# Fifteen and fourteen of 22 pairs by seven products, sums of activations made during `up`, and moves by GpSimd's queue

## The chip, the core and the metric

The kernel runs on one core of one Trainium2 chip. The metric is the device time of one execution in microseconds; what the host does to lay out arrays before the launch is not part of it. Five engines work beside one another, each on its own list of instructions in order: TensorE (PE; its weight loads are shown as PEld), VectorE (DVE), ScalarE (ACT), GpSimd (POOL) and SyncE (SP). DMA transfers are issued from the lists of SP, ACT or GpSimd and carried by 16 DMA engines that all of them share. TensorE writes to PSUM; the other operands lie in SBUF, 128 partitions wide.

## The reference

One encoder block on x of 256 tokens by 2048 features, in float32:

```python
hn = rmsnorm(h, mix_norm_pre)
z, xbc, dt_raw, u = split(hn @ w_in)                 # 2048 -> 1024, 1536, 32, 1024
mix = concat([ssd_mixer(z, xbc, dt_raw, ...), pool_mixer(u, ...)]) @ w_out
h = h + rmsnorm(mix, mix_norm_post)
gate, val = split(rmsnorm(h, ffn_norm_pre) @ w_up)   # 2048 -> 2 x 5632
ff = (gelu(dwconv(gate)) * val) @ w_down             # 5632 -> 2048
h = h + rmsnorm(ff, ffn_norm_post)
h = h + rmsnorm(sigmoid(rmsnorm(h, ple_norm_pre) @ w_ple_gate) * (p @ w_ple), ple_norm_post)
```

All six large weights together are 204 MB in float32, each read once or, in parts, twice.

## The kernel before

**Precision.** Every large product is made of three: an operand is split into a high part in the reduced float32 format that TensorE takes (`hi`, a cast on ScalarE, L152) and the rest (`lo`, a subtraction on VectorE, L153); the sum hi·hi + hi·lo + lo·hi is accumulated. `split` does this for 1024 columns of weights at a time, into a ring of five pairs of buffers. The raw weights come through a ring of three buffers of 1 MiB (`raw`). Larger tiles (128 x 2048, 1 MiB) come from one pool of 13 `page`s, half-size ones from three `mid`s.

**Stages.** In order: `dtu` (part of `w_in`), `xbc`, `z` with the two mixers between, `wo` (`w_out`), `up` (11 groups `s` of 512 gate and 512 value columns), `dn` (`w_down`, two halves of 1024 columns, 22 pairs of 128 rows each), `gt` (the gate, two halves, 8 pairs each), and the end. `up` computes features by tokens (`feature_pairs`: 64 matmuls per call, an l.h.s. of high weights with 512 columns of activations, high and low side by side, then low weights with 256). `dn` and `gt` compute tokens by features (`token_major`): a regular pair is 2 k-tiles x 2 token halves x 2 column halves x 3 products = 24 matmuls of 512 columns.

**Seven products.** For the pairs named in `fast`, `seven_products` (L239) does the 2 x 2 block product of a pair by seven block products instead of eight (Winograd's form): 21 matmuls. It needs sums of the activations' blocks, `s1` to `s4` (`pair_sums`, L774: four small VectorE operations, a cast, a subtraction), and sums of the weights' blocks (`add_blocks`, L232: three additions). After the last fast pair `combine` (L269) puts the seven accumulators together. In `dn` the fast pairs are 12 of 22 in each half; in the gate 2 of 8 in each.

**What is made ahead.** The block sums of the weights of all these 28 pairs are made during `up`, by `block_sums`: `fetch` loads the pair (1 MiB) into a page, `add` makes the sums two slots later, `store` writes them to device memory in the slot after. A slot is one half of a `feature_pairs` call; `work` is the list of jobs per slot, and `aside()` runs the next entry. Two of the 28 stay in SBUF. In `dn` a fast pair then loads the three raw blocks it still needs (0.75 MiB) and, unless held, its block sums (1 MiB, tile `dn..t`). The sums of activations are made in `dn` itself by `hid_sums`, just before they are used: at each fast pair of the first half, and again in the second but for four pairs (`dn_keep`), whose sums stay in two pages.

**Order and queues.** The instructions of each engine follow the program's text, shifted where a planner finds them ready earlier. All loads and stores are on SP's queue (`load`, L119), in program order, apart from the very first two (ACT's) and the low half of the gate's first block, which GpSimd's queue adds onto a negated copy (`first_gate`, L943). `at` tells before which pair of the second half of `dn` the residual `h` is loaded back (`back`, 13) and that block is prepared (`first_gate`, 16). In `up` GpSimd multiplies the convolved gate by the token factors `rfb` (L885), 11 times.

Of the kernel before, what the change touches and what calls it, by code (L numbers as in the profile page):

```python
# [51 lines left out]
def build(nc, a, out):  # L52
    x = a["x"][0]
    w_in, w_out, w_up = a["w_in"][0], a["w_out"][0], a["w_ffn_up"][0]
    w_down, w_gate, w_ple = a["w_ffn_down"][0], a["w_ple_gate"][0], a["w_ple"][0]
    out = out[0]

    with tile.TileContext(nc) as tc, \
# [37 lines left out]
        c_dt = DSSD + 1536  # L96
        r0 = wp.tile([P, 2048], F32, tag="raw", bufs=3, name="dtur0")
        for n in range(2):
            first = ins(nc.scalar.dma_start(r0[:, n * 352:(n + 1) * 352],
                                            w_in[:P, c_dt + n * 352:c_dt + (n + 1) * 352]))  # L100
# [55 lines left out]
        def raw(name, src, a_, b_):  # L156
            r = wp.tile([P, 2048], F32, tag="raw", bufs=3, name=name)
            if src is None:
                return r
            last["dma"] = load(r[:, :a_ * b_].rearrange("p (a b) -> p a b", a=a_), src, True)  # L160
            return r
# [46 lines left out]
        def block_sums(name, w, c0, k, held):  # L208
# [30 lines left out]
        def seven_products(name, stage, w, k0, c0, a_, acc, alt, start, stop):  # L239
# [3 lines left out]
            if (stage, c0, k0) in sums_:  # L243
                r = raw(f"{name}r", None, 0, 0)
                last["dma"] = load(r[:, 512:1536], w[(k0 + 1) * P:(k0 + 2) * P, c0:c0 + 1024], True)
                last["dma"] = load(r[:, :512], w[k0 * P:(k0 + 1) * P, c0:c0 + 512], True)
# [6 lines left out]
            else:  # L253
                r = t = raw(f"{name}r", w[k0 * P:(k0 + 2) * P, c0:c0 + 1024]
                            .rearrange("(k p) c -> p k c", p=P), 2, 1024)
# [35 lines left out]
        def token_major(name, w, c0, ks, get, acc, tail=1, fast=(), alt=None, sums=None, at=()):  # L291
# [3 lines left out]
            for u in range(nu):  # L295
# [3 lines left out]
                if u in fast:  # L299
                    if u == fast[0]:  # L300
# [3 lines left out]
                r = None if f"{name}{k0}_0" in ready else raw(f"{name}r{k0}", w[k0 * P:(k0 + 2) * P, c0:c0 + 1024]  # L304
                                                               .rearrange("(k p) c -> p k c", p=P), 2, 1024)
# [17 lines left out]
        def feature_major(name, w, c0, get, acc):  # L323

            for u in range(4):
                r = raw(f"{name}r{u}", w[u * 512:(u + 1) * 512, c0:c0 + 512]
                        .rearrange("(k p) c -> p k c", p=P), 4, 512)
# [12 lines left out]
        def feature_pairs(name, w, c0, get, acc):  # L340
# [102 lines left out]
        for u in range(0, NK, 2):  # L443
            r = [wp.tile([P, 2048], F32, tag="raw", bufs=3, name=f"dtur{u}") if u else r0, page(f"dtur{u + 1}")]
            for j in range(2):
                k = u + j
                if k == 0:
                    last["dma"] = load(r[0][:, 704:1056], w_in[:P, c_dt + 704:c_dt + 1056])
# [3 lines left out]
                for c0, c1 in ((0, 704), (704, 1056)) if k == 1 else ((0, 1056),):  # L452
                    last["dma"] = load(r[j][:, c0:c1], w_in[k * P:(k + 1) * P, c_dt + c0:c_dt + c1])
# [59 lines left out]
        load(pmat.rearrange("p (g s t) -> p g s t", g=4, s=2),  # L513
# [565 lines left out]
```

## Time and profile before

| what | value |
|---|---|
| median of 3 runs | 1123.38 us (1123.28 to 1124.6) |
| profiled execution, its time | 1123.11 us |
| profiled execution, its span (first to last instruction) | 1121.3 us |
| granted TensorE clock, mean | 0.997 |
| DMA | 300.87 MB, 268 GB/s over the span |

A row of a group reads: line of the kernel, engine, operation, output<-inputs by tile name, shapes, count | busy us, mean ns of one | idle time of the engine just before, and what ended it. A row by stretches reads: stretch in us, its length, busy time and number of instructions for PE, PEld, DVE, ACT and POOL, then granted clock, mean busy share of the 16 DMA engines, and GB/s. In the chain of work, a piece is start, length, engine, tile and line. A row of a DMA issue has its size and the time from issue to landing. Matmuls are pipelined: one of 512 columns is shown as about 393 ns long, but starts 231 ns after the one before it.

### The profile page before, as it was taken

The page shows a single profiled execution, that of the slowest core. Times are in us where ns is not written, and L with a number is a line of the kernel's source. Part 1 is how long each engine was busy: PE and PEld are TensorE (multiplying, and loading weights), DVE is VectorE, ACT ScalarE, POOL GpSimd, SP SyncE. Part 2 cuts the span into 40 slices and gives each one's busy share as a digit, 9 for nine tenths or more (in the row PEclk, how much of TensorE's full clock was granted, in tenths as well). Part 3 has the DMA queues.
Part 4 walks back from the last instruction along what each step waited for, and adds up shares of the span by engine and source line. Part 5 has one row for each costly group of instructions (what it writes and reads, how often), then busy time and mean ns, then how long its engine had stood idle before and what let it go on. Part 6 is the DMA issues. An engine that isn't in the chain of part 4 may idle for free.

```text
span 1121.3 us, 15775 instructions
## 1 busy us (share of the span) xinstructions
PE 1109.1 (99%) x5971; PEld 956.4 (85%) x5971; DVE 925.2 (83%) x1275; ACT 663.9 (59%) x927; POOL 76.2 (7%) x86
## 2 busy tenths in 40 slices
PE   9999999999999999999999999999999999999996
PEld 9999987888888888888888888888888888888875
DVE  6569895799898877877877768888899999889795
ACT  6847663555764554554545445445677777786672
POOL 0200004200110100000000000000000000001001
PEclk9999999999999999999999999999999999999998
DMA  9862447456789989989999898996969688995663
GB/s 363 310 207 96 170 161 269 151 188 190 252 308 347 328 300 336 314 289 309 333 330 314 276 330 289 325 304 224 339 185 334 221 286 301 383 318 177 230 235 109
DMA packets 145996, 300.87 MB, mean 268 GB/s; under 512 B 5504, under 2 KB 98560, under 8 KB 137856
## 3 DMA queue, kind: packets, MB, share of 16 engines
q1 hardware_dynamic: 145360, 298.45, 78.6%
q0 software_dynamic: 272, 1.05, 0.5%
q8 instruction: 47, 0.77, 0.3%
q10 hardware_dynamic: 288, 0.36, 0.1%
q14 instruction: 29, 0.24, 0.1%
HBM read 268.38 MB, written 31.46 MB: 267 GB/s over the span
## 4 chain that ended last, share of the span: by engine, by line
PE 96%; ACT 1%; DVE 1%; issue 1%; POOL 1%; POOLq 0%; DVEq 0%; ACTq 0%
PE va L87 22%; PE ga L87 21%; PE dna L87 14%; PE woa L87 7%; PE xbc L87 6%; PE gt L87 5%; PE dtu L87 4%; PE z L87 4%; PE dns L87 3%; PE dn0s L87 1%; PE dn1s L87 1%; PE ple L87 1%; PE pw L87 1%; PE yd L87 0%; PE gts L87 0%
## 5 line engine op out<-in xcount | busy, mean ns | idle before, releaser
L87 PE MATMUL ga<-wox,ug_0h 128*128 128x512 f32 x352 | 125.5, 395 | 0.0
L87 PE MATMUL ga<-wox,ug_1h 128*128 128x512 f32 x352 | 125.1, 394 | 0.0
L87 PE MATMUL va<-wox,uv_1h 128*128 128x512 f32 x352 | 124.8, 393 | 0.0
L87 PE MATMUL va<-wox,uv_0h 128*128 128x512 f32 x352 | 124.8, 393 | 0.0
L87 PE MATMUL ga<-wox,ug_1l 128*128 128x256 f32 x352 | 99.1, 282 | 0.0
L87 PE MATMUL ga<-wox,ug_0l 128*128 128x256 f32 x352 | 99.1, 282 | 0.0
L87 PE MATMUL va<-wox,uv_1l 128*128 128x256 f32 x352 | 99.1, 281 | 0.0
L87 PE MATMUL va<-wox,uv_0l 128*128 128x256 f32 x352 | 99.1, 281 | 0.0
L87 PEld LDWEIGHTS va<-wox,uv_1h 128*128 128x128 f32 x352 | 66.1, 188 | 15.0
L87 PEld LDWEIGHTS va<-wox,uv_0h 128*128 128x128 f32 x352 | 66.1, 188 | 15.0
L87 PEld LDWEIGHTS ga<-wox,ug_0h 128*128 128x128 f32 x352 | 66.1, 188 | 14.9
L87 PEld LDWEIGHTS ga<-wox,ug_1h 128*128 128x128 f32 x352 | 66.1, 188 | 14.9
L87 PEld LDWEIGHTS ga<-wox,ug_0l 128*128 128x128 f32 x352 | 66.2, 188 | 0.1
L87 PEld LDWEIGHTS ga<-wox,ug_1l 128*128 128x128 f32 x352 | 66.2, 188 | 0.0
L87 PEld LDWEIGHTS va<-wox,uv_0l 128*128 128x128 f32 x352 | 66.2, 188 | 0.0
L87 PEld LDWEIGHTS va<-wox,uv_1l 128*128 128x128 f32 x352 | 66.2, 188 | 0.0
L885 POOL TENSOR_TENSOR fc<-fc,rfb 128x1024 f32<-128x1024 f32 x11 | 28.0, 2547 | 438.6 <-ACT fc L884 438.6
L87 PE MATMUL dna<-dn_0h,hs 128*128 128x512 f32 x160 | 50.1, 393 | 0.0
L87 PE MATMUL dna<-dn_1h,hs 128*128 128x512 f32 x160 | 49.9, 393 | 0.0
L235 DVE TENSOR_TENSOR dnb<-dnb 128x1024 f32<-128x1024 f32 x24 | 30.8, 1283 | 17.8 <-DMA dnb<-w_ffn_down 17.6
L903 ACT CAST hs<-hid 128x512 fp32r<-128x512 f32 x44 | 27.2, 617 | 23.2 <-PE dna L87 14.8
L904 DVE TENSOR_TENSOR hs<-hid,hs 128x512 fp32r<-128x512 f32 x44 | 30.2, 686 | 9.8 <-ACT hs L903 9.7
(1903 smaller groups left out, 3105.3 us busy)
## 6 DMA issues: line engine op xcount, KB each, us to landing
dnb<-w_ffn_down SPq DMA_DIRECT2D x24, 1024.0 KB, 10.4
dns<-dnb SPq DMA_DIRECT2D x22, 1024.0 KB, 7.4
dn0r<-w_ffn_down SPq DMA_DIRECT2D x10, 1024.0 KB, 6.0
dn1r<-w_ffn_down SPq DMA_DIRECT2D x10, 1024.0 KB, 7.1
zr<-w_in SPq DMA_DIRECT2D x8, 1024.0 KB, 5.1
dtur<-w_in SPq DMA_DIRECT2D x14, 528.0 KB, 8.7
wo0r<-w_out SPq DMA_DIRECT2D x7, 1024.0 KB, 5.6
wo1r<-w_out SPq DMA_DIRECT2D x6, 1024.0 KB, 5.5
```

The source lines that it names most:

```text
L87: last["pe"] = ins(nc.tensor.matmul(o, lhsT, rhs, start=start, stop=stop, skip_group_check=True))
L235: nc.vector.tensor_add(v[:, 0:2], v[:, 0:2], v[:, 1::2])
L885: nc.gpsimd.tensor_tensor(cv.rearrange("p (f t) -> p f t", f=4), cv.rearrange("p (f t) -> p f t", f=4), rfb.unsqueeze(1).to_broadcast([P, ...
L903: nc.scalar.copy(t[:, :512], src)
L904: nc.vector.tensor_sub(t[:, 512:], src, t[:, :512].bitcast(F32))
```

## The change

1. **More fast pairs.** `dn`: 15 pairs in the first half and 14 in the second by seven products; the gate: three in the first half and two in the second, five in all. In the gate's second half the order of the pairs is changed, so that its two fast pairs are two whose activation sums were made in the first half. There are now 34 pairs whose block sums are made in `up`; the spacing of these jobs goes from 3 slots to 2.4.
2. **Sums of activations made during `up`.** For ten pairs (`dn_stored`) `hid_sums_jobs` makes the sums as soon as the activations are there, in a job of `work`, and stores them to device memory (0.5 MiB each). In both halves of `dn` they are loaded into a `mid`. The other pairs' sums are made in `dn`, in both halves; no pages hold sums any more.
3. **GpSimd's queue.** `load_aside` issues from GpSimd's queue: fetches and stores of block sums, stores and loads of the sums of activations.
4. **Host tiles.** All large weights, `pool_w` and the pool matrix are laid out on the host as the tiles that are loaded: 128 rows of 8 KB each, one after another (`up` loaded rows of 1 KB, `xbc` 2 KB, the others 4 KB). The three raw blocks of a fast pair are parts of such a tile, rows of 4 and 2 KB.
5. **Order inside a fast pair.** The block sums' second half (`t42`) is split before the first (`t13`), and the products are in the order a11, a12, a22, s4, s2, s1, s3 (before: a11, a12, s4, s1, s3, a22, s2).
6. **Moved steps.** The multiplication by `rfb` in `up` goes from GpSimd to VectorE. In `dn`, `back` goes to pair 18, the first gate block is loaded at 19 (a step of its own, `first_load`) and prepared at 21. The pages of `vg` are taken when first written.

```diff
+        def load_aside(dst, src, ahead=True):
+            with tc.issue_after(last["dma"]) if not ahead else nullcontext():
+                return ins(nc.gpsimd.dma_start(dst, src))
...
 def block_sums(name, w, c0, k, held):
             def fetch():
                 r = page(f"{name}b{c0}_{k}")
                 pg.append(r)
-                load(r.rearrange("p (k c) -> p k c", k=2),
-                     w[k * P:(k + 2) * P, c0:c0 + 1024].rearrange("(k p) c -> p k c", p=P))
+                load_aside(r, w[c0 // 1024, k // 2], False)
...
-                    load(t, pg[0])
+                    load_aside(t, pg[0])
...
 def seven_products(name, stage, w, k0, c0, a_, acc, alt, start, stop):
-                last["dma"] = load(r[:, 512:1536], w[(k0 + 1) * P:(k0 + 2) * P, c0:c0 + 1024], True)
-                last["dma"] = load(r[:, :512], w[k0 * P:(k0 + 1) * P, c0:c0 + 512], True)
+                last["dma"] = load(r[:, 512:1536], w[c0 // 1024, k0 // 2][:, 1024:], True)
+                last["dma"] = load(r[:, :512], w[c0 // 1024, k0 // 2][:, :512], True)
...
+            t42 = split(f"{name}d", t[:, 1024:], 1024)
             t13 = split(f"{name}c", t[:, :1024], 1024)
-            t42 = split(f"{name}d", t[:, 1024:], 1024)
             for x, (wh, wl), c, o, own in (
-                    ("a11", b11, 0, alt[0], True), ("a12", b2, 0, acc[0][0], False), ("s4", b2, 512, acc[0][1], False),
-                    ("s1", t13, 0, alt[1], True), ("s3", t13, 512, alt[2], True), ("a22", t42, 0, acc[1][0], False),
-                    ("s2", t42, 512, alt[3], True)):
+                    ("a11", b11, 0, alt[0], True), ("a12", b2, 0, acc[0][0], False), ("a22", t42, 0, acc[1][0], False),
+                    ("s4", b2, 512, acc[0][1], False), ("s2", t42, 512, alt[3], True), ("s1", t13, 0, alt[1], True),
+                    ("s3", t13, 512, alt[2], True)):
...
 def feature_pairs(name, w, get, acc):
-                r = raw(f"{name}r{u}", w[u * 1024:(u + 1) * 1024, c0:c0 + 256]
-                        .rearrange("(k p) c -> p k c", p=P), 8, 256)
+                r = raw(f"{name}r{u}", w[u])
...
-        dn_fast, gt_fast, dn_keep = ((2, 3, 5, 7, 8, 10, 12, 13, 15, 16, 18, 19), (2, 3, 5, 7, 8, 10, 12, 13, 15, 16, 18, 19)), ((4, 6), (1, 2)), (3, 8, 13, 18)
-        gt_ks = list(range(NK)), [0, 1, 12, 13, 8, 9, 2, 3, 4, 5, 6, 7, 10, 11, 14, 15]
+        dn_fast, gt_fast = ((2, 3, 4, 5, 6, 8, 9, 10, 11, 13, 14, 15, 16, 18, 19), (2, 3, 4, 5, 6, 8, 9, 10, 13, 14, 15, 16, 18, 19)), ((4, 5, 6), (1, 2))
+        dn_stored = (2, 3, 4, 6, 9, 10, 13, 15, 16, 19)
+        gt_ks = list(range(NK)), [0, 1, 8, 9, 10, 11, 2, 3, 4, 5, 6, 7, 12, 13, 14, 15]
...
-                work[3 * i + 2 + j].extend(jobs)
+                work[12 * i // 5 + 3 + j].extend(jobs)
...
+        def hid_sums_jobs(k):
+            o = []
+            def make():
+                o.append(lp.tile([P, 1024], F32R, tag="hs", bufs=2, name=f"he{k}"))
+                hid_sums_of(k, o[0][:, 512:].bitcast(F32), o[0])
+            def store():
+                kept[k] = dp.tile([P, 1024], F32, tag=f"hsum{k}", bufs=1, name=f"hsum{k}")
+                load_aside(kept[k], o[0].bitcast(F32))
+            return [make], [store]
+        for u in dn_stored:
+            for j, jobs in enumerate(hid_sums_jobs(2 * u)):
+                work[u // 2 * 8 + u % 2 * 2 + 6 + j].extend(jobs)
...
-            nc.gpsimd.tensor_tensor(cv.rearrange("p (f t) -> p f t", f=4), cv.rearrange("p (f t) -> p f t", f=4),
+            nc.vector.tensor_tensor(cv.rearrange("p (f t) -> p f t", f=4), cv.rearrange("p (f t) -> p f t", f=4),
                                     rfb.unsqueeze(1).to_broadcast([P, 4, L]), op=ALU.mult)
...
 def hid_sums(k):
             (h1, l1), (h2, l2) = get_hid(k), get_hid(k + 1)
-            if k not in kept:
...
+            o = mid(f"hd{k}", F32R)
+            if k in kept:
+                load_aside(o.bitcast(F32), kept[k])
+                d = sums_in(o)
             else:
-                d = kept[k]
+                d = hid_sums_of(k, mid(f"hs{k}"), o)
...
+        def first_load():
+            first["r"] = page("gtf")
+            last["dma"] = load(first["r"], w_gate[0, 0])
...
-                      fast=dn_fast, sums=hid_sums, at={13: back, 16: first_gate})
+                      fast=dn_fast, sums=hid_sums, at={18: back, 19: first_load, 21: first_gate})
```

More of the change, by code (lines that the diff above doesn't have):

```diff
@@ L154, in split, with raw @@
             return hi, lo
-        def raw(name, src, a_, b_):
+        def raw(name, src=None):
             r = wp.tile([P, 2048], F32, tag="raw", bufs=3, name=name)
-            if src is None:
-                return r
-            last["dma"] = load(r[:, :a_ * b_].rearrange("p (a b) -> p a b", a=a_), src, True)
+            if src is not None:
+                last["dma"] = load(r, src, True)
             return r
@@ L871, in build, with hid_part, hid_sums_of @@
             for j, jobs in enumerate(block_sums(*w_, i >= len(which) - 2)):
-                work[3 * i + 2 + j].extend(jobs)
-        hid = []
+                work[12 * i // 5 + 3 + j].extend(jobs)
+        hid, kept = [], {}
+        def hid_part(k):
+            return hid[k // 8][:, (k % 8) * L:(k % 8 + 2) * L]
+        def hid_sums_of(k, s, o):
+            return pair_sums(f"he{k}", s, o, *(hid_part(k)[:, i * P:(i + 1) * P] for i in range(4)))
+        def hid_sums_jobs(k):
[10 more added lines that the diff above has]
+                work[u // 2 * 8 + u % 2 * 2 + 6 + j].extend(jobs)
         for s in range(DFF // 512):
@@ L941, in back @@
                 last["dma"] = load(h[t], h_kept[t])
+        first = {}
+        def first_load():
+            first["r"] = page("gtf")
+            last["dma"] = load(first["r"], w_gate[0, 0])
         def first_gate():
-            r, hi, lo = page("gtf"), page("gtfh", F32R), page("gtfl", F32R)
-            src = w_gate[:2 * P, :1024].rearrange("(k p) c -> p k c", p=P)
-            last["dma"] = load(r.rearrange("p (k c) -> p k c", k=2), src)
+            r, hi, lo = first["r"], page("gtfh", F32R), page("gtfl", F32R)
             nc.scalar.activation(lo, r, AF.Copy, scale=-1.0)
-            nc.gpsimd.dma_start(lo.rearrange("p (k c) -> p k c", k=2), src, accum_op=ALU.add)
+            nc.gpsimd.dma_start(lo, w_gate[0, 0], accum_op=ALU.add)
             nc.scalar.copy(hi, r)
@@ L963, in build @@
         gple = gload("gple", a["ple_norm_post"][0])
-        vg = [page(f"vg{t}") for t in range(2)]
+        vg = []
         sq = [[], []]
@@ L1023, in build @@
                         nc.scalar.activation(so, sv, AF.Square, accum_out=q)
+                    if half == n == 0:
+                        vg.append(page(f"vg{t}"))
                     nc.vector.tensor_mul(vg[t][:, c], v, gple[:, c])
```

77 lines of the change are left out of this document (38 added, 39 removed).

## The prediction

> **What bounds the kernel now.** I read the page first: the share of each engine and the chain of work that ended last.
>
> ```profile
> span 1121.3 us, 15775 instructions
> PE 1109.1 (99%) x5971; PEld 956.4 (85%) x5971; DVE 925.2 (83%) x1275; ACT 663.9 (59%) x927; POOL 76.2 (7%) x86
> DMA packets 145996, 300.87 MB, mean 268 GB/s; under 512 B 5504, under 2 KB 98560, under 8 KB 137856
> ...
> PE 96%; ACT 1%; DVE 1%; issue 1%; POOL 1%; POOLq 0%; DVEq 0%; ACTq 0%
> ```
>
> TensorE carries 96% of the chain, so a microsecond is gained by fewer matmuls, and lost by any new wait in front of one. The busy share of PE alone would not prove that it streams, so the second view is the chain in order of time (start, length, what):
>
> ```profile
> 319.91 22.33 PE va L87 x128
> ...
> 809.75 5.55 PE dna L87 x24
> ...
> 891.49 22.16 PE dna L87 x96
> ```
>
> A regular pair of `down` is 24 matmuls of 512 columns in 5.55 us; 96 take 22.16 us. One costs 0.231 us. The third view is the table by stretches: `up`, the two column halves of `down`, then two stretches of 20 us with high DMA traffic (columns: length, then busy time of PE, PEld, DVE, ACT, POOL, granted clock, DMA share, GB/s).
>
> ```profile
> 319.91:788.96 469.05, 469.05 (x2689) 411.74 (x2689) 378.05 (x479) 235.24 (x312) 28.01 (x11) 1.00 0.93 307
> 788.96:902.50 113.54, 113.54 (x493) 92.27 (x493) 105.23 (x146) 81.69 (x108) 0.00 (x0) 1.00 0.77 261
> 902.50:1016.74 114.24, 114.19 (x495) 92.40 (x494) 104.81 (x143) 84.60 (x109) 3.82 (x8) 1.00 0.91 323
> 960.00:980.00 20.00, 20.00 (x88) 16.26 (x87) 18.60 (x27) 14.84 (x18) 0.00 (x0) 1.00 0.97 372
> 20.00:40.00 20.00, 20.00 (x126) 20.00 (x125) 14.35 (x19) 15.56 (x21) 4.88 (x3) 1.00 1.01 398
> ```
>
> Each half of `down` has 12 fast pairs (21 matmuls) and 10 regular ones: 492 matmuls, 492 x 0.231 = 113.7 us, and the halves last 113.5 and 114.2 us. `Down` has no room between matmuls. But VectorE is busy 105 of 114 us beside it, and in the second half the DMA engines 91%: the cover over the cheaper matmuls is thin there, and this is where the change adds work.
>
> **The change, part by part.**
>
> *Fewer matmuls.* Fast pairs go from 12 and 12 to 15 and 14 in `down`, and from 4 to 5 in the gate: 6 more, each saving 3 matmuls: 18 x 0.231 = 4.16 us, all on the chain. Half 0 of `down` becomes 15 x 21 + 7 x 24 = 483 matmuls, 111.7 us; half 1 14 x 21 + 8 x 24 = 486, 112.4 us. The order of the seven products adds no matmul: 0.
>
> *VectorE in down.* Rows of VectorE in `down`, and some in order of time (start, length):
>
> ```profile
> L904 DVE TENSOR_TENSOR hs<-hid,hs 128x512 fp32r<-128x512 f32 x41 | 28.1, 686 | 9.1 <-ACT hs L903 9.0
> L153 DVE TENSOR_TENSOR dn_0l<-dn1r,dn_0h 128x1024 fp32r<-128x1024 f32 x10 | 12.2, 1219 | 2.2 <-ACT dn_0h L152 2.2
> L782 DVE TENSOR_TENSOR he<-hd,he 128x512 fp32r<-128x512 f32 x15 | 10.2, 683 | 0.7 <-ACT he L781 0.7
> ```
>
> ```profile
> 809.85 1.22 DVE L153 TENSOR_TENSOR dn010bl<-dn010r,dn010bh 128x1024 fp32r<-128x1024 f32 x1
> 810.99 0.68 DVE L904 TENSOR_TENSOR hs<-hid,hs 128x512 fp32r<-128x512 f32 x1
> 811.59 1.22 DVE L153 TENSOR_TENSOR dn010cl<-dn010t,dn010ch 128x1024 fp32r<-128x1024 f32 x1
> 812.72 0.28 DVE L777 TENSOR_TENSOR hd<-hid 128x128 f32<-128x128 f32 x1
> 812.93 0.28 DVE L778 TENSOR_TENSOR hd<-hid 128x128 f32<-128x128 f32 x1
> ```
>
> Instructions overlap at their ends: from start to start 1024 columns take 1.14 us, 512 take 0.60, 128 take 0.21 (0.31 behind a result just made). A regular pair costs 2 x 1.14 + 0.60 = 2.88 us of VectorE; a fast pair whose sums are at hand 0.60 + 3 x 1.14 + 0.60 = 4.62, under its 21 x 0.231 = 4.85 us of PE; one whose sums are made there about 1.5 more (four small ones and one of 512), 6.15, which is over. So "made" pairs live on the slack of others. Before: half 0 12 x 6.15 + 10 x 2.88 = 102.6 us, half 1 (four sums kept) 96.5. After, with ten pairs' sums loaded: 10 x 4.62 + 5 x 6.15 + 7 x 2.88 = 97.1 and 10 x 4.62 + 4 x 6.15 + 8 x 2.88 = 93.8. VectorE gets lighter by 5.5 and 2.7 us while PE loses 2.1 and 1.4: the cover holds, 0. ScalarE follows it at 82 to 85 of 114 us busy.
>
> *What up takes on.* Ten `pair_sums` at 1.5 us; block sums of 34 instead of 28 pairs; eleven multiplications by `rfb`, moved from GpSimd.
>
> ```profile
> L885 POOL TENSOR_TENSOR fc<-fc,rfb 128x1024 f32<-128x1024 f32 x11 | 28.0, 2547 | 438.6 <-ACT fc L884 438.6
> L235 DVE TENSOR_TENSOR dnb<-dnb 128x1024 f32<-128x1024 f32 x24 | 30.8, 1283 | 17.8 <-DMA dnb<-w_ffn_down 17.6
> ...
> dnb<-w_ffn_down SPq DMA_DIRECT2D x24, 1024.0 KB, 10.4
> dns<-dnb SPq DMA_DIRECT2D x22, 1024.0 KB, 7.4
> ```
>
> VectorE: 10 x 1.5 + 6 x (1.14 + 2 x 0.60) + 11 x 1.14 = 15 + 14 + 12.5 = 41.5 us, on 378 busy of 469: 420, 89%. PE covers it: 0, if the multiplication, which now waits for the Gelu in VectorE's own queue, finds splits ahead of it (between 0 and, at one of its 1.14 us for each of 11 groups, 12.5; I take 0, as the five buffers of split weights hold 5 x 16 matmuls, 14 us by the `va` row of 128 in 22.33). VectorE waited 17.6 us for fetched blocks in all and PE for none of it.
>
> *Queues.* 34 fetches, 32 stores, ten stores and twenty loads of sums pass SP's queue for GpSimd's, 96 issues. In `up` GpSimd then runs nothing else; SP's loads of weights no longer stand behind a fetch that waits for a page. Of GpSimd's queue there is one DMA in the trace, the low half of the gate's first block:
>
> ```profile
> gtfl<-w_ple_gate POOLq DMA_DIRECT2D x1, 1024.0 KB, 14.4
> ...
> gtf<-w_ple_gate SPq DMA_DIRECT2D x1, 1024.0 KB, 13.0
> ...
> dn126r<-w_ffn_down SPq DMA_DIRECT2D x1, 512.0 KB, 11.7
> ```
>
> 14.4 us there against 13.0 for its high half on SP in the same busy stretch. The same 1024 KB take SP 7.4 to 10.4 us in the rows above, so the queue costs between 0 and 7 us of landing time each; I take 1.4, the pair nearest to each other. In `up` a block is fetched two slots, 11 us, before its sum, and the wait that replaces it is VectorE's, covered as above. In `down` a load of sums must find a free buffer of three, two pairs (9.7 us) ahead: covered at 7 to 10 us, not at 14.
>
> *Host tiles.* `up` moves 307 GB/s at a share of 0.93, which is 330 at full share, most of it in rows of 1 KB (98560 packets are under 2 KB). The change adds 12 block moves of 1 MiB and ten of half: 17.8 MB, 38 GB/s, 345 in all: more than 330. Were the rows to stay, `up` would be bound by DMA. They become 8 KB; the stretch from 20 to 40 us, with rows of 4224 B, has 394 at full share. 345 fits: 0. The start (352 columns at a time, as before) is taken as unchanged: between -1 and +1 us, 0.
>
> *DMA in down.* A regular pair loads 1 MiB, a fast one 1.75 (0.75 if its block sum is held), loaded sums 0.5. Check on before: half 1 is 10 + 12 x 1.75 + 2 (`h` back) + 2 (gate) + 1 (`ple`) = 36 MiB, 37.7 MB, in 114.2 us: 330 GB/s, and the row has 323. After: half 0 7 + 13 x 1.75 + 2 x 0.75 + 5 = 36.25 MiB, 340 GB/s. Half 1: 8 + 24.5 + 5 + 2 + 2 + 1 = 42.5 MiB, 44.6 MB, in 112.4 us: 396 GB/s. The highest rows are 372 and 398; half 1 as it stands has 323 / 0.91 = 355 at full share. So the sum is close: at 398 it costs 0, at 372 (119.9 us) 7.5, at 355 13.2. I take 0.3, because not all is due inside the half. Three raw buffers mean that pairs 2 to 4 are loaded when pair 2 starts; from there 33.75 MiB, 35.4 MB, are left for 101 us: 350 GB/s, and 364 if all must land 4 us before use. That lies under 372, and more of it moves in 8 KB rows than before.
>
> *The later gate block.* `h` comes back at pair 18 instead of 13, the first gate block is fetched at 19 and split at 21 (both were 16).
>
> ```profile
> 978.41 1.91 ACT L948 ACTIVATE gtfl<-gtf 128x2048 fp32r<-128x2048 f32 x1
> 980.63 1.43 POOL L949 DMA_DIRECT2D gtfl<-w_ple_gate  x1 [203.62 <-ACT gtfl L948]
> 1005.26 0.39 PE L87 MATMUL dna<-dn_0h,hs 128*128 128x512 f32 x1
> 1022.92 0.63 PE L87 MATMUL gt<-gtfh,dnxh 128*128 128x512 f32 x2
> ```
>
> Now: pair 20 starts at 1005.3 and the gate at 1022.9. After, 3.5 us earlier (five of the six pairs): 1001.8, 1019.4. ScalarE ran this copy some 6 us ahead of pair 16; ahead of pair 21 (1007.3) that is about 1001, GpSimd issues at 1003, and with 14.4 us it lands at 1017.5, 2 us before use, where it had 28. Two copies of 1.9 us now stand on ScalarE in front of pair 21's splits. Between 0 and 5 us (a landing of 20); I take 0.1.
>
> *Gate 5.* One more fast pair makes three in a row (4, 5, 6) in the gate's first half: VectorE does four splits for two and makes one more pair's sums, 4.0 + 2.1 - 2.3 = plus 3.9 us, against PE minus 0.7, once. Around these pairs the table by stretches has
>
> ```profile
> 1034.00:1064.00 30.00, 30.00 (x132) 24.41 (x131) 22.62 (x32) 20.88 (x27) 1.85 (x6) 1.00 0.70 233
> ```
>
> 7.4 us of VectorE free: between 0 and, with no gap at the right place, 3.9 - 0.7 = 3.2; I take 0.1.
>
> *Sum.* -4.16 + 0.3 + 0.1 + 0.1 = -3.7. Span 1121.3 - 3.7 = 1117.6; the profiled run took 1123.11 us: 1119.4; the median of the three runs, 1123.38, is 0.27 above it: 1119.7.
>
> **The rivals.**
>
> *Down's second half is bound by DMA (slower).* For it: 396 GB/s asked on average, pairs 13 to 16 fast in a row with `h` and the gate block right behind, and landing times that already reach 11.7 us for half a MiB. Against: the stock of three raw buffers, PE without a gap at 372. At 372 for the whole half it is +7.5: 1127; it turns the sign under 44.6 / (112.4 + 4.2) = 383 GB/s if nothing is loaded ahead. The Trainium skill ("SBUF — State Buffer", "Summary: rules for kernel authors") says to reckon with about 358 GB/s for transfers from HBM. By that rule half 1 would take 124.6 us, +12.2, an estimate from that page. This case's trace does not hold to it: 372 and 398 stand above. Chance 0.17.
>
> *GpSimd's queue is late.* Loads of sums that take 14.4 us where 9.7 are given cost up to 4.7 each; the ones that stand third in a row of fast pairs, about six, cost up to 28. For it: one row of 14.4; against: that one reads and adds, at twice the size. With 1.5 each: 1128.7. The Trainium skill, in the same section of "SBUF — State Buffer", says that descriptor making for this queue is starved while VectorE is in one of its fast modes; the single row here, an issue of 1.43 us, shows no such delay. Chance 0.07.
>
> *The gate starts late.* The low half lands at 20 us: +3: 1122.7, no change that can be measured. Chance 0.12.
>
> **How the numbers follow.** My forecast, the stages keep their cover: 0.64, its own range 1117.7 to 1121.1. A measurement of this kernel tells 0.2% (2.2 us) from no change. Faster: 0.64 plus a small part of the late gate, 0.66; same: the rest of it, 0.10; slower: DMA and the queue, 0.24. The range of 8 in 10 starts at 1117.6 (start gains, no waits) and reaches to the DMA case at 1127.
>
> **What would show it.** Right: no gap between matmuls in `down`, halves of 111.7 and 112.4 us, `up` at a lower DMA share than 0.93 with more GB/s, VectorE there near 89%. Wrong: ScalarE waiting for `dn..t` or `dn..r` in half 1 with a DMA share over 1 (DMA); matmuls or `hd` behind a GpSimd DMA (queue); the first `gtfl` matmul alone in a gap at the gate (late block); a stretch of `up` longer than its 469 us, that VectorE or DMA has no cover there.

## The result and the profile after

The changed kernel takes 1142.29 us (1141.3 to 1143.9), the kernel before beside it on the same chip 1123.33: ratio 1.017, 95% interval 1.0158 to 1.0183. The profiled execution took 1142.01 us, span 1140.2, 18.9 more than before. The forecast was 3.7 less. The page of the changed kernel (engines, DMA, shares of the chain):

```profile
span 1140.2 us, 15963 instructions
...
PE 1112.3 (98%) x5953; PEld 955.1 (84%) x5953; DVE 939.8 (82%) x1317; ACT 671.4 (59%) x939; POOL 100.0 (9%) x171
DMA packets 57389, 333.90 MB, mean 293 GB/s; under 512 B 6368, under 2 KB 7264, under 8 KB 23520
...
PE 69%; DMA 13%; DVE 9%; issue 4%; ACT 3%; POOL 1%; DVEq 0%; POOLq 0%; ACTq 0%
```

TensorE had 96% of the chain and has 69%: transfers and VectorE now decide for stretches. The table by stretches (`up`, then about the two halves of `down`; columns as in the prediction):

```profile
319.75:801.00 481.25, 473.88 (x2691) 414.38 (x2690) 394.05 (x547) 235.10 (x321) 40.64 (x76) 0.99 0.89 342
801.00:914.00 113.00, 112.38 (x488) 91.13 (x488) 102.90 (x132) 86.17 (x110) 5.91 (x11) 1.00 0.88 322
914.00:1034.00 120.00, 114.47 (x485) 89.80 (x484) 102.25 (x125) 86.16 (x106) 6.77 (x13) 1.00 0.94 352
```

From the first matmul of one stage to the first of the next, the span splits as follows (us):

| stretch | before | forecast | after |
|---|---|---|---|
| `up` (first `va` to first `dn`) | 469.0 | 469.0 | 481.2 |
| `down`, `ple` and panel (to the first `gt`) | 234.1 | 231.1 | 239.3 |
| gate and end | 98.4 | 97.8 | 100.0 |

`Up` lost 12.1 us; `down` should have lost 3.5 us of matmuls and got 8.7 us of gaps; the end should have lost 0.7 and got 2.3. Three views show where `up` went: groups of VectorE there, issues (us to landing), and GpSimd's waits in `up` (total, times, longest).

```profile
L237 DVE TENSOR_TENSOR dnb<-dnb 128x1024 f32<-128x1024 f32 x28 | 34.1, 1221 | 30.9 <-DMA dnb<-w_down 30.9
...
dnb<-w_down POOLq DMA_DIRECT2D x29, 1024.0 KB, 15.3
...
POOL dns L123 <- DVE dnb L239: 236.0, 23, 39.1
POOL hsum L123 <- DVE he L780: 131.9, 10, 29.3
```

From 320 to 790 us GpSimd stands 368 us in front of these *stores*, which wait for VectorE. The fetches are behind them in the same list, as its instructions in order of time show:

```profile
486.99 1.60 POOL L123 DMA_DIRECT2D dnb<-w_down  x3
524.93 0.54 POOL L123 DMA_DIRECT2D dns<-dnb  x1 [36.33 <-DVE dnb L239]
528.73 0.54 POOL L123 DMA_DIRECT2D dns<-dnb  x1 [3.27 <-DVE dnb L239]
529.26 1.07 POOL L123 DMA_DIRECT2D dnb<-w_down  x2
```

Three fetches go out at once, and the next one 42 us after the first of them. These three land after 13.4, 17.9 and 22.3 us; the median of all is 15.3 (10.4 before). Then VectorE, in order itself, stands at the addition with the next split of weights behind it. The chain at the largest gap, 3.6 us:

```profile
640.93 0.46 POOL dns L123
641.39 0.06 issue
641.46 12.61 DMA gtb<-w_gate
...
655.92 1.15 DVE uv_1l L157
657.06 0.04 issue
657.11 9.98 PE va L88 x47
```

The store at 640.93 released the fetch, the fetch the addition at 654.09, and behind that came the split `uv_1l` on which TensorE stood. The other two large gaps in `up`, 2.1 us at 379 and 1.3 us at 562, have the same chain of store, fetch, addition and split. In `down` the gaps are of two kinds, a load of sums, and ScalarE's copies of the gate's first block in front of pair 19's splits (`dn138`; tiles bear the first row block, twice the pair):

```profile
939.05 8.55 DMA hd<-hsum
...
1011.15 1.91 ACT L970 ACTIVATE gtfl<-gtf 128x2048 fp32r<-128x2048 f32 x1
1012.97 0.60 ACT L156 CAST dn138ah<-dn138r 128x512 fp32r<-128x512 f32 x1
1013.47 1.04 ACT L156 CAST dn138bh<-dn138r 128x1024 fp32r<-128x1024 f32 x1
1014.43 1.90 ACT L972 CAST gtfh<-gtf 128x2048 fp32r<-128x2048 f32 x1
1016.22 1.04 ACT L156 CAST dn138dh<-dn138t 128x1024 fp32r<-128x1024 f32 x1
```

Gaps of 0.8 and 1.9 us stand behind the loads at 833 and 946 us, and about 5 us of gaps between 1011 and 1030 us.

### The profile page after: what moved, and what is told of

Read it like the earlier page. It is cut to its first block, busy times and chain, and to the rows that moved or that the text cites. A ratio compares the mean times of both kernels' runs of the same rounds, so it can differ in the third digit from the quotient of the medians.

```text
span 1140.2 us, 15963 instructions
## 1 busy us (share of the span) xinstructions
PE 1112.3 (98%) x5953; PEld 955.1 (84%) x5953; DVE 939.8 (82%) x1317; ACT 671.4 (59%) x939; POOL 100.0 (9%) x171
## 4 chain that ended last, share of the span: by engine, by line
PE 69%; DMA 13%; DVE 9%; issue 4%; ACT 3%; POOL 1%; DVEq 0%; POOLq 0%; ACTq 0%
PE dna L88 12%; PE ga L88 11%; PE va L88 9%; DMA dnb<-w_down 8%; PE woa L88 7%; PE xbc L88 6%; PE gt L88 5%; PE dtu L88 4%; PE z L88 4%; PE dns L88 3%; PE dn0s L88 2%; DMA hd<-hsum 1%; PE dn1s L88 1%; DMA uv41r<-w_up 1%; DMA uv21r<-w_up 1%
## 5 line engine op out<-in xcount | busy, mean ns | idle before, releaser
L88 PE MATMUL va<-wox,uv_1h 128*128 128x512 f32 x352 | 127.3, 399 | 0.0
L421 ACT ACTIVATE fc<-gr,vt 128x256 f32<-128x256 f32 x44 | 24.1, 595 | 74.1 <-DVE gr L909 74.1
L237 DVE TENSOR_TENSOR dnb<-dnb 128x1024 f32<-128x1024 f32 x29 | 35.3, 1221 | 30.9 <-DMA dnb<-w_down 30.9
L88 PE MATMUL dna<-dn_0h,hs 128*128 128x512 f32 x120 | 37.4, 394 | 0.9 <-DVE hs L930 0.9
L88 PE MATMUL dna<-dn_1h,hs 128*128 128x512 f32 x120 | 38.3, 393 | 0.0
## 6 DMA issues: line engine op xcount, KB each, us to landing
dnb<-w_down POOLq DMA_DIRECT2D x29, 1024.0 KB, 15.3
```

The lines of the kernel that those rows point to most:

```text
L88: last["pe"] = ins(nc.tensor.matmul(o, lhsT, rhs, start=start, stop=stop, skip_group_check=True))
L237: nc.vector.tensor_add(v[:, 0:2], v[:, 0:2], v[:, 1::2])
L421: nc.scalar.activation(o, i, AF.Identity, bias=vec(bcol + f), scale=vec(wcol + half * wstep + f))
```

## The experiments

Times are medians against the kernel before on the same chip; "down" is from the first `dn` matmul to the first of the gate, in the profiled execution.

### Which part of the queue costs: four edits of the changed kernel

**All of it back on SP.** In `fetch`, `store` and the store of sums `load_aside(...)` becomes `load(...)`; in `hid_sums` `last["dma"] = load(..., True)`.

> The changed kernel with all 96 issues of block sums and of sums of activations back on SP's queue; the rest (29 fast pairs in down, host tiles, sums of activations made during up, gate 5) as changed. Theory 1, GpSimd's queue: fetches stand in it behind stores that wait for VectorE, come late and in bunches, and VectorE, in its own order, stands at the addition with the next split behind it. Then up falls from 481.2 back to about 469 us, the gaps of TensorE at 833 and 945 us (0.8 and 1.9 us, loads of sums in down) go too, and the time is 1142.3 - 12 - 3 = about 1127; the gaps at the end of down's second half stay. Theory 2, too much work for VectorE in up (sums of activations, 34 blocks, the multiplication by rfb): up stays over 477 us with gaps, and the time over 1137. Theory 3, SP's queue is blocked in its turn by fetches that wait for a page: gaps in front of which loads of raw weights come last, up between 470 and 480.

Measured: 1153.24 us, ratio 1.0272 (1.0252 to 1.0291), `up` 485.0, down 247.7. Theory 1 in this form is wrong, and theory 3 comes nearest, with `up` longer still than it said. The two gaps in front of loads of sums in `down` did go, as theory 1 said; others came, as in the run below with the loads on SP.

**Only `up`'s issues back on SP.** As above, without `hid_sums`.

> Only what is issued in up (fetches and stores of block sums, stores of sums of activations) goes back to SP's queue; the loads of sums in down stay on GpSimd's. Theory 1 (the queue): up about 469 us, down as changed (113.0 and 120.0 us with its gaps), time about 1130, 3 us over the kernel with everything on SP if the gaps at 833 and 945 us are due to the queue of those loads. If these gaps come from the wait for a free buffer and not from the queue, both kernels take the same. Theory 2 (VectorE's work): over 1137.

Measured: 1151.48 us, 1.0246 (1.0223 to 1.0269), `up` 487.0. SP's waits in `up`, and SP's instructions in order of time:

```profile
SPq L118 <- DVE he L780: 98.9, 10, 12.8
...
615.08 0.33 SPq L118 DMA_DIRECT2D ug71r<-w_up  x1
625.95 0.33 SPq L118 DMA_DIRECT2D hsum<-he  x1
626.36 0.38 SPq L118 DMA_DIRECT2D dns<-dnb  x1
626.80 0.79 SPq L118 DMA_DIRECT2D dnb<-w_down  x1
627.64 1.18 SPq L118 DMA_DIRECT2D ug71r<-w_up  x1
```

The same fault on the other queue: of the raw weights `ug71r`, issued as two halves, the second half leaves 12.6 us after the first, behind stores that wait for VectorE, and a gap of 2.1 us follows at 638.7.

**Only the stores back on SP.**

```diff
-                    load_aside(t, pg[0])
+                    load(t, pg[0])
...
-                load_aside(kept[k], o[0].bitcast(F32))
+                load(kept[k], o[0].bitcast(F32))
```

> Only the stores (block sums and sums of activations) go back to SP's queue; fetches and the loads of sums in down stay on GpSimd's. This parts two forms of theory 1. If fetches are late because they stand behind stores in an in-order queue, up is about 469 to 471 us and the time about 1130 to 1132, as with all of up on SP. If GpSimd's queue itself is slow (15.3 us from issue to landing instead of 10.4), fetches still land late, and up stays over 475 us, the time over 1136. A third outcome: stores on SP wait there for VectorE and hold up the raw weights; then scalar splits wait for loads and up is longer than 481 us.

Measured: 1130.74 us, 1.0066 (1.0051 to 1.0081): 11.6 us back from 42 stores moved (32 of block sums, ten of sums of activations). The stretch of `up`, VectorE's group, issues, the longest of GpSimd's waits in it, SP's wait for the sums of activations, and two rows of SP in order of time:

```profile
319.65:788.75 469.10, 469.10 (x2691) 411.75 (x2689) 394.40 (x547) 237.27 (x321) 15.35 (x29) 1.00 0.92 350
...
L237 DVE TENSOR_TENSOR dnb<-dnb 128x1024 f32<-128x1024 f32 x28 | 33.8, 1217 | 2.3 <-DMA dnb<-w_down 2.3
...
dnb<-w_down POOLq DMA_DIRECT2D x29, 1024.0 KB, 10.2
...
POOL dnb L123 <- DMA dns<-dnb: 118.7, 9, 20.5
...
SPq L118 <- DVE he L780: 18.3, 10, 2.9
...
609.96 6.20 SPq L118 DMA_DIRECT2D uv70r<-w_up  x2
...
618.98 0.33 SPq L118 DMA_DIRECT2D hsum<-he  x1
```

`Up` has no gap, with the same work on VectorE (394 us busy in both). Fetches on GpSimd's queue land after 10.2 us; the same tiles fetched by SP in the run before landed after 9.5. So the queue itself is 0.7 us slower there, and the loss came from what stood in front of the fetches. SP now has the stores between the raw weights, and no gap follows: without the fetches in its list both halves of `uv70r` are issued ahead of the same store behind which they stood in the run before, and SP waits 18.3 us for the ten stores of sums in place of 98.9. What costs is fetches and stores in one list, GpSimd's or SP's. In the kernel before, with both on SP 3 slots apart, no gap came; which of the closer spacing, the six more blocks and the stores of sums made the difference on SP was not tried. The Trainium skill ("DMA: Bandwidth & Descriptors", "Issuing engines are not separate DMA queues") says that issuing from several engines saves only the time of the issue itself. Here the choice of list for 42 stores was worth 11.6 us, because an issue that waits holds up all behind it.

**The multiplication by `rfb` back on GpSimd** (L912, `nc.vector` becomes `nc.gpsimd`).

> The changed kernel with the multiplication by rfb back on GpSimd (11 of 2.5 us there, 11 of about 1.14 us off VectorE). Theory 2 (VectorE's work in up) expects a good part of the 12 us back: up 470 to 476 us, time under 1137. Theory 1 (the queue) expects VectorE's 12.5 us to lie in its idle time: up 480 to 483 us, time 1141 to 1144, or somewhat longer, as GpSimd now stands at the Gelu with fetches and stores behind it.

Measured: 1156.28 us, 1.0297 (1.0265 to 1.0329), `up` 493.1. Theory 2 expected a good part of the 12 us back, and 14 us were lost instead. By itself this run does not decide, because the move also put a wait for ScalarE's Gelu in front of GpSimd's stores and fetches; the run before does, with the same work on VectorE and no gap. GpSimd's waits in `up` have a new row:

```profile
POOL fc L912 <- ACT fc L911: 133.8, 10, 25.1
```

### The queue alone in the kernel before

`load_aside` for fetches and stores, and L885 on `nc.vector`, in the kernel before; nothing else.

> The kernel before, with one part of the change alone: fetches and stores of its 28 block sums on GpSimd's queue (3 slots apart, as it has them), and the multiplication by rfb on VectorE, so that GpSimd does not stand at the Gelu. Theory (in-order queue, stores that wait for VectorE in front of fetches): gaps in up here too, but with 3 slots a fetch behind a waiting store has more time; up 470 to 478 us, the time 1124 to 1133. If the queue alone is harmless at this spacing, the time is 1123.3, and the loss in the changed kernel needs both the queue and the closer spacing with its 34 blocks.

Measured: 1151.17 us, 1.0245 (1.0213 to 1.0276); `up` 495.5. The theory holds in kind, but the price is far above the 10 us at most that it gave. Its chain, and GpSimd in order of time:

```profile
384.46 18.18 DMA ug20r<-w_ffn_up
...
383.51 2.11 POOL L124 DMA_DIRECT2D dnb<-w_ffn_down  x3
```

Three fetches go out together, and a raw load issued at the same time takes 18.2 us to land (raw loads of `up` in the kernel before: 8.3 in the median, 14.1 at most). A gap of 4.7 us stands behind it, so at this place the bunch hurts in a second way, through the DMA engines. So 28 blocks, 3 slots apart, are enough for a loss, with the old rows of 1 KB in `up`.

### `down`: loads of sums

**A scratch tile** (with the stores on SP).

```diff
-                d = hid_sums_of(k, mid(f"hs{k}"), o)
+                d = hid_sums_of(k, sp.tile([P, 512], F32, tag="junk", bufs=1, name=f"hs{k}"), o)
```

The expectation's "pair 12" and "pair 8" are the numbers in the tile names, pairs 6 and 4.

> Stores on SP's queue (as in e3_stores_sp), and in down the four small sums of a pair that is made there go to a scratch tile of 512 columns of their own instead of one of the three mids, so that the loads of stored sums find a free mid a pair earlier. Theory: the gaps of TensorE in front of the sums of pair 12 in either half (0.9 us at 821, 2.9 us at 933 in e3_stores_sp) come from the load being issued only when pair 8's last matmul lets go of a mid, 8 to 10 us of landing before use. Then both gaps go, and the time is 1130.7 - 3.8 = about 1127. Rival: the landing itself is late (GpSimd's queue, or DMA traffic in half 1); then the gap of half 1 stays at 2 us or more and the time at 1129 or more.

Measured: 1130.1 us, 1.0053 (1.0034 to 1.0072). Both gaps are gone and down falls from 240.5 to 236.8 us, 3.7 of the 3.8 expected: a mid that is free a pair earlier is enough to remove them. The time missed its mark because `up` now had a gap of 3.4 us (stretch 474.1). The chain there:

```profile
718.08 8.92 DMA gts<-gtb
...
727.57 8.71 DMA dnb<-w_down
...
738.12 1.15 DVE uv_1l L157
```

A page is let go when a store has landed; only then does the next fetch start, and VectorE waits for it with a split behind. The size varies: this kernel's five executions took 1125.6 to 1131.5 us.

**Wider spacing at the end of `up`** (with both edits above).

```diff
-                work[12 * i // 5 + 3 + j].extend(jobs)
+                work[(9 * i // 4 + 3 if i < 20 else 48 + 13 * (i - 20) // 5) + j].extend(jobs)
```

> As f1_scratch (stores on SP, scratch tile in down), and the jobs of block sums spaced 2.25 slots apart for the first 20 pairs and 2.6 after, instead of 2.4 throughout. In f1_scratch one gap is left in up, 3.4 us at 736 (6.5 to 7 in two other runs), behind a chain store, fetch, addition: 10 us until the store of one block has landed and lets go of its page, 10 more for the fetch into it. Theory (pages): the 13 pages are shared with the activations of up, which take one more every 16 slots, and the last blocks are short of them; spaced wider there, the gap goes or falls under 1 us, up is 469 to 470 us and the time about 1125. Rival (DMA traffic): 2.25 slots ask for more at the start of up, gaps come there instead, and the time stays at 1128 to 1132.

Measured: 1125.47 us (1124.9 to 1125.92 in ten executions), 1.0018 (1.0008 to 1.0027). `Up` is 469.04 us without a gap, and the spread is gone. A later kernel with the same spacing had a gap of 4.3 us at 643.6 in one execution, so the shortage is rarer, not shown to be over.

**The loads on SP instead** (stores on SP, no scratch tile).

> Stores on SP's queue, and the loads of stored sums in down too; only the 34 fetches are left on GpSimd's queue. If the loads are late because of the queue, the gaps at 821 and 933 us shrink and the time is about 1127. If they are late because of the free mid, the gaps stay, and what stands behind the waiting load on SP (raw weights) comes late too: more gaps in down, time 1131 to 1140.

Measured: 1133.0 us, 1.0085 (1.007 to 1.01), down 242.3. It is neither outcome. The gaps in front of the sums of pair 6 ("pair 12" by its tile) are gone, as the first said. In either half the load is still issued right behind pair 4's last matmul, but lands after 3.7 and 3.9 us; on GpSimd's queue (with the stores alone on SP) it took 7.6 and 9.6. The medians of all twenty are 5.6 and 8.2. So those gaps needed both, a mid that comes free late and a slow landing on GpSimd's queue. Whether that queue is slower in itself, or its loads share the DMA engines with raw loads that SP issues beside them, stays open. The time is the second outcome's: SP now waits 29.5 us for VectorE's last step of a pair's sums and 22 us for matmuls, waits that its list in `down` did not have with the stores alone on it. New gaps of 0.6 and 1.4 us stand behind block sums that took 9.1 and 15.9 us to land. In `up`, spaced as before, one gap of 2.4 us is left.

### `down`: the end of the second half

**The gate's block earlier**, `at={13: back, 15: first_load, 17: first_gate}`, without and with the scratch tile (both with stores on SP, at the old spacing):

> Stores on SP's queue, and h loaded back at pair 13, the gate's first block loaded at 15 and prepared at 17 of down's second half (18, 19 and 21 in the changed kernel). Theory: the gaps from 1000 to 1018 us (about 6 us with the half clock behind them) come from the two copies of 1.9 us that ScalarE makes behind the late block, in front of the splits of pairs 19 and 20. With the block earlier the copies lie beside fast pairs with stock, the gaps go, and the time is 1130.7 - 6 = about 1125. Rival (DMA): half 1 asks for 44.6 MB in 112 us, and what comes earlier displaces raw weights; then gaps appear from pair 13 to 19 at a DMA share over 0.97, and the time is 1128 to 1135.

> Both of the last two edits with the stores on SP's queue. If the three causes (stores in GpSimd's queue, free mids, late copies) are all there is, no gap over 0.5 us is left in up and down, and the time is the prediction's sum, 1119 to 1121. If DMA binds down's second half, it stays at 1124 or more with waits for raw weights in half 1.

Measured: 1138.5 us, 1.0101 (1.0065 to 1.0137), and 1126.23, 1.0034 (1.0018 to 1.005). The profiled executions have gaps of 7.0 and 6.5 us behind late fetches in `up`, so only down is read: 240.7 and 236.0 us, against 240.5 and 236.8 without the edit. The gap behind the copies moved from pair 19 to pair 15, and down is hardly shorter for it. Earlier is no cure.

**One copy on GpSimd** (on top of the spacing; L970 becomes a multiplication by -1.0 there).

> As g1_front, and the negated copy of the gate's first block (1.9 us of ScalarE) is made by GpSimd, which is idle in down. Theory: the gaps from 1001 to 1019 us come from the two copies on ScalarE in front of pair 19's splits; with one of two gone they fall by half, 2 to 3 us, and the time is 1122 to 1123. Rival (what is late is the loads of pair 19, 14 us in the changed kernel): no change against g1_front within 1 us.

Measured: 1128.14 us, 1.0042 (1.0027 to 1.0057), 2.7 slower than without. The reason is in neither theory; VectorE and GpSimd in order of time:

```profile
994.10 4.33 DVE L157 TENSOR_TENSOR dn136dl<-dn136t,dn136dh 128x1024 fp32r<-128x1024 f32 x1 [0.26 <-ACT dn136dh L156]
...
993.38 5.72 POOL L970 TENSOR_SCALAR gtfl<-gtf 128x2048 fp32r<-128x2048 f32 x1 [10.48 <-DMA gtf<-w_gate]
```

A subtraction of 1.22 us took 4.33: it lies within GpSimd's 5.72 us. The Trainium skill ("SBUF — State Buffer", "Who interferes with whom") says that a VectorE instruction with two SBUF inputs and a GpSimd one that reads SBUF shut each other out for the whole instruction. The row agrees that they do, though the subtraction ends 0.7 us before GpSimd's recorded end. In the kernel before, the eleven multiplications by `rfb` agree in full: the VectorE instruction beside each ends 0.5 to 1.1 us after GpSimd's end, nearly its whole usual length.

**No preparation ahead**, `at={18: back}`.

> As g1_front, and the gate's first block is not prepared ahead at all: no copies, no load of it during down; the gate loads and splits its first pair as any other. The same theory: no gap over 0.5 us from 1001 to 1012 us, down's second half 5 to 6 us shorter than in g1_front; the gate starts 1 to 4 us later instead. Rival (loads of pair 19 late, or VectorE full): the gaps of pair 19 stay.

Measured: 1126.75 us, 1.0027 (1.0017 to 1.0036). Down is 233.3 us, 3.1 less than with the copies (236.4); the gate loses 2.5 again in a gap at its start. So the preparation, copies and the block's loads together, is the greater part of those gaps; 5 to 6 was too much.

**The order of the copies.** `first_load` at 20; then load at 19 and the copies under `tc.issue_after(last["act"])`, at 20; then that with `back` at 14 and the load at 18.

> As g1_front, and the gate's first block is loaded a pair later, at 20, behind the loads of pair 19, so that its two copies stand on ScalarE behind all splits of pair 19. Theory (copies in front of pair 19's splits): the gaps from 998 to 1004 us (3.5 us in g1_front) go; the block then lands late, and the splits of pair 20 behind the copies may wait for it: gaps of 0 to 3 us there. Time 1121.5 to 1124. Rival (loads of pair 19 late): no change.

> As g1_front, with the block loaded at 19 as there and its copies only ordered on ScalarE behind the last split of pair 19. Theory: the gaps from 998 to 1004 us go, and as the block has long landed, pair 20's splits do not wait for it; the gate's low half is issued 5 us later and lands at about 1014, before the gate starts at 1021. Time 1121 to 1122.5, less than the kernel before. Rival (loads of pair 19 late, or VectorE behind): 1125 as g1_front.

> As h8_copies_after, with h loaded back at pair 14 and the gate's block at 18, so that these 3 MiB do not stand on SP in front of pair 18's and 19's loads. If what is left at the end of down's second half is loads that come late there, 1 to 2 us less than h8_copies_after; if DMA is short from pair 13 to 16 (four fast pairs in a row), 1 to 4 us more.

Measured: 1124.46 us, 1.001 (1.0 to 1.0019); 1125.95, 1.0028 (1.0018 to 1.0039); 1126.24, 1.0024 (1.0015 to 1.0034). In all three pair 19's gaps shrink to 0.8 to 1.3 us, and one of 2.1 us appears at pair 20, in front of which the copies now stand. So neither place nor landing is the whole of it: some 2 us of the 3.8 of ScalarE show wherever they stand; my next theory was that ScalarE and VectorE have no lead left there, that is, no splits made ahead of the matmuls. Taking `h` out of these loads' way did not help.

**One fast pair less in the second half** (on top of the spacing, with `first_load` at 20): without pair 19; without 16; without 19, the load at 19 and the copies under `issue_after` at 20.

> As h4_load20 (stores on SP, scratch tile, wider spacing, the gate's block loaded at 20), with one fast pair less in down's second half: pair 19 by the regular product, 13 fast pairs, 33 block sums. It costs 3 matmuls, 0.69 us. Theory: ScalarE and VectorE have no lead left at the end of the half, so that the two copies, 3.8 us of ScalarE, show wherever they stand behind a fast pair; behind a regular pair, with some 1.5 us more slack each, the gap of 2.1 us at 1003 goes: 1122.5 to 1123.5. Rival: the lead is lost in the run of pairs 13 to 16; then the gap stays and the time is 1125.

> As h4_load20, with pair 16 instead of pair 19 by the regular product, so that three fast pairs stand in a row instead of four, and 18 and 19 stay. If the lead is lost in the run of four, the gaps of pairs 19 and 20 shrink by more than the 0.69 us this costs: 1122.5 to 1123.5. If the copies cost their time behind pair 19 in any case, 1125.

> As k1_13fast, with the gate's block loaded at 19 and its copies ordered on ScalarE behind the splits of pair 19, one pair of regular products more ahead of the gate: the block has landed when its copies start, and the low half lands before the gate. 1121.5 to 1123; if load and order make no difference, as k1_13fast.

Measured: 1123.12 us, 1.0001 (0.9992 to 1.0011); 1121.92, 0.9992 (0.9982 to 1.0001); 1124.97, 1.0018 (1.0009 to 1.0028). Breaking the run of four fast pairs (13 to 16) gains 2.5 us net of 0.69 for matmuls, more than giving up pair 19 (1.3): most of the lead is lost ahead of pair 18. That it is the row of four, and not just one fast pair fewer ahead, was not tried. The last one missed: its copies stand in front of pair 20's splits too, and it has a gap of 1.5 us at 998. The chain there goes through three additions of `combine` on VectorE, 0.7 us each, that stand in front of the split of pair 19; in the first of the three kernels, without this gap, two of them stand behind it. The kernel without 16, ScalarE in order of time and its table from `down` to the gate:

```profile
998.85 1.92 ACT L970 ACTIVATE gtfl<-gtf 128x2048 fp32r<-128x2048 f32 x1
1000.67 1.90 ACT L972 CAST gtfh<-gtf 128x2048 fp32r<-128x2048 f32 x1
...
789.17:914.00 124.83, 124.83 (x544) 101.68 (x543) 112.20 (x142) 93.75 (x121) 5.81 (x11) 1.00 0.89 328
914.00:1021.50 107.50, 106.39 (x465) 86.08 (x463) 95.50 (x119) 82.06 (x103) 7.48 (x17) 1.00 0.95 357
```

One gap of 1.2 us is left. It is the fastest of all, 1.4 us under the median beside it, and its interval still touches no change: no version here is shown to be faster than the kernel before.

## Why the prediction was wrong, step by step

- *Queues* failed, the step that the sum takes at 0. It priced a GpSimd DMA by its landing time and put the rest away with "a block is fetched two slots, 11 us, before its sum, and the wait that replaces it is VectorE's, covered as above". Two things were left out. Fetch and store of different blocks share one list, and the store waits for VectorE, so a fetch does not leave two slots ahead but when the store in front of it is done. And VectorE's wait is not covered by its idle time: the next split of weights stands behind the addition. Measured: 11.6 us (the stores moved alone). The rival "GpSimd's queue is late" had the loads in `down` only; those landed after 8.2 us in the median with the stores on SP, not 14.4, and cost 2.7 us in the changed kernel. Either a mid that is free earlier or SP's queue removes these gaps. That VectorE's work holds that queue up does not show either: with the stores on SP the fetches land after 10.2 us beside a VectorE that is 84% busy.
- *Fewer matmuls* was right: in the kernel with wider spacing the first half of `down` runs without a gap, 111.4 us from its first matmul to the first of the second half (113.6 before), against 111.7 forecast.
- *What up takes on* was right in its result: `up` is 469.1 us when the stores are away. Its size was off: VectorE gained 16 us, not 41.5, and is 84% busy, not 89%. In the kernel before, one VectorE instruction beside each of the eleven multiplications on GpSimd is stretched, together by 15.7 us over the median of their form (summed from the trace), and that went away with the move. Some 9 us of the difference are left open.
- *VectorE in down, the cover holds* was half right. The first half runs without a gap once the mids suffice. At the end of the second it fails: the sum compared averages over a half, and the lead is used up by the time that pairs 18 and 19 come, behind four fast pairs in a row.
- *The later gate block* failed in its size, 0.1 taken. It said that the copies stand "in front of pair 21's splits"; the planner put them before pair 19's, a fast one. The gate itself started without a wait, as forecast. Without the preparation `down` is 3.1 us shorter.
- *Host tiles* and *DMA in down* held: 350 GB/s at a share of 0.92 in `up`, 357 GB/s at 0.95 in the second half, where the fastest kernel has one gap, behind ScalarE's copies. The rival of a DMA-bound half did not come. With all 14 fast pairs (wider spacing) 41.4 of the 44.6 MB moved inside the half, in 115 us at 359 GB/s; the rest was loaded ahead.
- *Gate 5* held: with the stores on SP, gate and end take 97.8 us, as forecast. (Its 4.0 + 2.1 - 2.3 is 3.8, not 3.9, which changes nothing.)
- Not in the sum: 2.1 us at the very end, told below.

So the sum's -3.5 and -0.7 of matmuls are there, and against them stand 12.1 us in `up`, 8.7 of gaps in `down`, and 2.3 at the end. What stays open: why the shortage of pages shows in some executions and not in others, and what the last gaps of the second half would be without `combine` behind the last fast pair.

## What to carry to other kernels

An engine's list is a queue for waits: before moving a DMA to another list, write down what each issue there waits for and what then stands behind it. Fetches and the stores that wait for compute belong on different lists here: stores between raw loads that are issued well ahead cost nothing, stores in front of fetches cost 12 us. "Covered" must be shown of the waiting instruction's successors, not of the engine's busy share. A cover that holds as an average over a stage can fail after several dense steps, and one-off work placed there shows.

## What the runs showed of the hardware

- GpSimd's `DRAIN` at the end gets longer with the DMAs that it has issued, by some 0.08 us each: 0.75 us with one (the kernel before), 2.4 with 21, 3.5 with 35, 5.2 with 55, 8.6 with 97. In the changed kernel it ended last, 2.1 us later than the end otherwise comes.
- A gap of TensorE can be followed by half clock, and that does not depend on its length alone. Stretches behind gaps of 2.1 and 3.6 us in the changed kernel, then of 2.9 and of 1.8 (with smaller ones behind it) with the stores on SP:

```profile
378.00:384.00 6.00, 4.06 (x18) 3.21 (x17) 6.00 (x10) 3.65 (x5) 0.00 (x0) 0.82 1.00 374
653.00:662.00 9.00, 5.61 (x24) 4.58 (x23) 7.91 (x11) 5.31 (x8) 0.00 (x0) 0.81 0.78 275
...
933.00:942.00 9.00, 6.28 (x28) 4.80 (x27) 7.29 (x13) 4.68 (x6) 0.53 (x1) 1.00 1.02 399
1003.00:1007.00 4.00, 3.78 (x10) 2.85 (x10) 2.22 (x3) 4.00 (x4) 1.67 (x3) 0.57 0.92 211
```

The third stays at 1.00. In the others the granted clock is 0.50 for 3.41 us: matmuls of 512 columns start 0.43 us after one another in place of 0.23, and some 1.7 us are lost. In every kernel with several such spells their starts lie whole multiples of 3.41 us apart (in the changed kernel 381.82 and 658.30 us, 81 times). So I divided each trace into windows of that length and summed TensorE's idle time in each. From `up` to the start of the gate, every window at full clock with 1.88 us or more of idle time is followed by half clock (25 windows, in 13 of the 20 kernels), and none with 1.87 or less is. The gap of 2.9 us above falls on two windows, with 1.5 and 1.4 us in them; the last, of 1.8 us with 0.5 behind it, lies in one.
